# Splitting the second mixer's weights by two GpSimd transfers

## The chip, the cores and the metric

The kernel runs on one core of one Trainium2 chip. The metric is device time in microseconds (us) of one execution; lower is better. Engines are named as in the profile: PE is TensorE (matmul), PEld its weight loads, DVE is VectorE, ACT is ScalarE, POOL is GpSimd, SP is SyncE, which in the kernel before issues every transfer. Each engine executes its own instructions in the order in which the program wrote them, and waits on semaphores for what it needs.

## The reference

A two-layer backbone over 256 context and 512 latent tokens of width 1024, all in float32. Each layer scales and shifts its input, runs a mixer, adds the gated result to the residual, normalises, and then does the same with a gated feed-forward of 2816 hidden units. The first layer's mixer is linear attention beside differential attention; the second layer's is a bidirectional state-space mixer, and that is where the change lies:

```
z, xbc, dt = split(hh @ w_in, (2048, 2048 + 2 * 4 * 128, 2 * 32))
xbc = silu(conv5(xbc, conv_w) + conv_b);  xs, B, C = split(xbc)
y   = ssd(forward) + flip(ssd(backward)) + d_skip * xs
y   = group_rms_norm(y * silu(z)) ;  out = y @ w_out
```

Its input weights w_in have 5184 columns of 1024 rows; its output weights w_out have 2048 rows of 1024 columns.

## The kernel before, in words

**Three matmuls for one.** Activations and weights are float32, and a matmul runs on a rounded form of it (float32r). So each operand is held as two rounded halves: hi, the rounded value, and lo, the rest. `mm3` adds hi by hi, hi by lo and lo by hi. The activations stand in R0 in both halves; the weights are split block by block as they are needed.

**The weight stream.** Every weight block of the whole kernel stands in one list, `plan`, in the order in which it is used. A block is 128 partitions by up to 1024 columns, 512 KB: 128 columns of an input matrix (eight row groups), half of a 256-column piece (`plan_halves`, the "z" blocks), or 128 rows of an output matrix (`plan_rows`). `issue_loads` (line 373) moves the stream: up to three blocks ahead it issues a load by SP into one of the three RAW buffers; and when fewer than four blocks are issued and not freed, it writes the high half of the next one by a ScalarE copy and the low half by a subtraction on VectorE or GpSimd, into slot j % 4 of RW. `take` hands a block to the matmuls, and `free` says that its slot can be used again.

**The order of the work.** A planner, `Timing` (line 34), carries a cost for each operation on each engine. Each operation is given a planned start from its operands' planned times and the engine's free time; at the end of a stretch (`flush`) everything is emitted in the order of planned starts, and that order is each engine's program. `tm.either` puts an elementwise operation on VectorE or GpSimd, whichever ends sooner by plan. Matmuls are emitted in the order in which the Python code asks for them; between them `pump` and `settle` let *chains* go on, which are Python generators that yield what they wait for: tiles, a PSUM bank (`single_free`, `pair_free`) or a condition.

**The second mixer.** `layer1` follows a written order of projections:

```
ORDER1 = "b0 x0 z0 x1 z1 x2 b1 z2 x3 x4 o0 x5 z3 b2 z4 o1 z5 x6 b3 x7 z6 o2 p z7 o3"
```

Here b is B and C of a group (two blocks, "cv"), x is the input of four heads (two blocks, "cv"), z the gate of four heads (two half blocks, taken and freed as a pair), o the output product of a group of eight heads (four blocks "sw", all held through it and freed during its last half tile), p the preparation of the following norm. Before b0 stands one block "dt". In all 1 + 24 + 16 + 16 = 57 blocks. A projection is followed on VectorE by the five-tap convolution (`conv_out`); `states` makes the chunk states from weighted inputs (XW) and B; `y_tile` makes the output of one 128-token tile for four heads, multiplies by the gate and transposes into the output slots OT; `out_tile` multiplies those by the output weights. `LN.chain` normalises and writes the next layer's input. HX holds, at different times, CB, XW and a piece of the gate, and the first half of it is the norm's scratch.

**Names that the change touches:** `Timing.dma` (line 209), `RW` (line 237), `single` and `single_free` (lines 272 to 276), `issue_loads` (line 373), `LN.chain` (line 628), `gla_mix` (its two kv pairs), and in `layer1` `states`, `y_tile` and `free_of`.

Of the kernel before, what the change touches and what calls it, by code (L numbers as in the profile page):

```python
# [12 lines left out]
F32R = mybir.dt.float32r  # L13
U8 = mybir.dt.uint8
AF = mybir.ActivationFunctionType
ALU = mybir.AluOpType
# [17 lines left out]
class Timing:  # L34
# [174 lines left out]
    def dma(self, out, src):  # L209
# [4 lines left out]
        self.note([out], [src], end + 0.95)  # L214
        self.put(t, self.nc.sync.dma_start, (out, src), {})


@with_exitstack
def backbone(ctx: ExitStack, tc: tile.TileContext, ins: dict, out: bass.AP):
# [14 lines left out]
    LNS = pool.tile([P, 2, 16], F32, name="LNS")  # L234
    ea64 = pool.tile([P, 1], F32, name="ea64")
    R0 = pool.tile([P, 2, KD, NTOK], F32R, name="R0")
    RW = pool.tile([P, 8, 1024], F32R, name="RW")
    R0f, RWf = R0.bitcast(F32), RW.bitcast(F32)
    NU = 24
    HB = pool.tile([P, NU * U], F32, name="HB")  # L240
# [24 lines left out]
    def pair():  # L265

        return min((PS[:, i:i + 2, 0:384] for i in pair_banks[0] if i not in held), key=tm.free)

    def pair_free():
        return tm.free(pair())  # L270

    def single():
        return min((PS[:, 2 + i, :] for i in range(6) if 2 + i not in held), key=tm.free)

    def single_free():
        return tm.free(single())

# [43 lines left out]
    def need(*cs):  # L323
        while not all(c.done for c in cs):
            need_one()
# [43 lines left out]
    def plan_halves(key, n, w, c0):  # L369
        for i in range(2):  # L370
            plan.append(((key, n, i), [(None, w[i * 512:(i + 1) * 512, c0:c0 + 256].rearrange("(k p) c -> p k c", p=P))], (4, 256)))

    def issue_loads(limit=None):
        limit = limit or len(plan)
        while wq["loaded"] < min(limit, wq["issued"] + 3):
            j = wq["loaded"]
            _, pieces, (a, b) = plan[j]
            rv = RAW[:, j % 3, 0:a * b].rearrange("p (a b) -> p a b", b=b)
            for sl, ap in pieces:
                dma(rv[:, :, sl] if sl is not None else rv, ap)  # L380
            wq["loaded"] += 1
        if wq["issued"] < min(limit, wq["freed"] + 4):
            j = wq["issued"]
            _, _, (a, b) = plan[j]
            r = RAW[:, j % 3, 0:a * b]
            i = j % 4
            hi, lo, hf = RW[:, i, 0:a * b], RW[:, 4 + i, 0:a * b], RWf[:, i, 0:a * b]
            if plan[j][0] in wgate:
                tm.either(r, r, wgate[plan[j][0]], ALU.mult)
            S.activation(hi, r, AF.Copy)  # L390
            tm.either(lo, r, hf, ALU.subtract)
            wviews[j] = hi.rearrange("p (a b) -> p a b", b=b), lo.rearrange("p (a b) -> p a b", b=b)
            wq["issued"] += 1
            issue_loads(limit)
# [184 lines left out]
    class LN:  # L579


        def __init__(self, l, w, acc, src, dst, nxt, tiles, xr, tmp, gate, gb, nhx=2, banks=(6, 7)):
            self.t0, self.nhx, self.banks = tiles[0], nhx, banks
            self.l, self.w, self.acc, self.src, self.dst, self.nxt = l, w, acc, src, dst, nxt
            self.xr, self.tmp, self.gate, self.gb = xr, tmp, gate, gb

        def load_gates(self):
            for m, g in self.gate.items():
# [31 lines left out]
        def chain(self, t):  # L620
# [27 lines left out]
            gg, bb = GB[:, nl, nw, m, 0, :], GB[:, nl, nw, m, 1, :]  # L648
            hx = HX[:, t % self.nhx, :].rearrange("p (k c) -> p k c", c=P)
            quick = t >= self.t0 + self.acc.shape[1] - 2  # L650
            c = slice(t * P, (t + 1) * P)
            for hf in range(2):
                ks = slice(4 * hf, 4 * hf + 4)
# [173 lines left out]
    def layer0(mslots, RA, pre):  # L827
# [115 lines left out]
        def gla_mix(h):  # L943
# [19 lines left out]
            yield kdT, v, pair_free  # L963

            kv = []
            for half in range(2):
                q = pair()
                for c in range(6 * half, 6 * half + 6):
                    p = slice(64 * (c % 2), 64 * (c % 2) + 64)
                    o = q[:, c % 2, (c % 6) // 2 * P:((c % 6) // 2 + 1) * P]  # L970
                    mm(o, tiles(kdT)[p, c // 2, :], vt[p, c // 2, :], True, True)
                    kv.append(o)
# [386 lines left out]
    def layer1(lnin, lnc):  # L1359
# [211 lines left out]
        def states(hg):  # L1571
            xs = XS[hg % 2]
            cs = {}

            def weighted(n):
                xw = XW[ring("xw", 2)]
                ds = {2: slice(0, 1), 5: slice(1, 2)}.get(n, slice(0, 2))
                nd = ds.stop - ds.start
                V.tensor_tensor(xw[:, ds], heads(xs[:, n, :]).unsqueeze(1).to_broadcast([P, nd, 4, 64]),
                                tq(n, 2, hg)[:, ds].unsqueeze(3).to_broadcast([P, nd, 4, 64]), ALU.mult)  # L1580
                return xw, ds

            def product(n, xw, ds):
                o = single()
                mm(o[:, ds.start * 256:ds.stop * 256], Bt[:, n, :], xw[:, ds].rearrange("p d h c -> p (d h c)"), True, True)
                cs[n] = o.rearrange("p (d c) -> p d c", d=2)

            def recur(d, i):
                seq = ((0, 1, 2, 3, 4), (1, 0, 5, 4, 3))[d]
                order = ((2, 2, 3, 4, 5), (5, 5, 4, 3, 2))[d]  # L1590
                s2 = ST[:, order[i] - 2, d, :]
                if i == 0:
                    S.activation(s2, cs[seq[0]][:, d, :], AF.Copy)
                    return
                s, n = ST[:, order[i - 1] - 2, d, :], seq[i]
                f, j = head_rows(seq[i])
                dv = EAL[:, f, d * 32 + hg * 4:d * 32 + hg * 4 + 4, j].unsqueeze(2).to_broadcast([P, 4, 64])
                tm.either(heads(s2), heads(s), dv, ALU.mult)
                V.tensor_tensor(s2, cs[n][:, d, :], s2, ALU.add)

            for ns, rs in (((0, 1), ((0, 0), (1, 0), (0, 1), (1, 1))), ((5, 2), ((1, 2), (0, 2))), ((4, 3), ((1, 3), (0, 3), (1, 4), (0, 4)))):
                w = [weighted(n) for n in ns]
                yield w[0][0], w[1][0], single_free
                for n, x in zip(ns, w):
                    product(n, *x)
                for d, i in rs:
                    recur(d, i)

        def y_tile(hg, t):
# [24 lines left out]
            tm.either(A, R[:, 1], cb.unsqueeze(1).to_broadcast([P, 4, P]), ALU.mult)  # L1634
            co = DS[:, n % 3, :]
            V.scalar_tensor_tensor(co, tq(t, 1, hg)[:, 1, :], cbd, DB[:, hg * 4:hg * 4 + 4], ALU.mult, ALU.add)
            yield A, ST[:, t - 2], single_free
            yd = single()[:, 0:256]
            for h in range(4):
                mm(yd[:, h * 64:(h + 1) * 64], A[:, h, :], xs[:, t, h * 64:(h + 1) * 64], True, True)  # L1640
            of = single()
            for d in range(2):
                mm(of[:, d * 256:(d + 1) * 256], cs, ST[:, t - 2, d, :], True, True)
            yo = R[:, 1].rearrange("p h i -> p (h i)")
# [5 lines left out]
            tm.either(tt, tt, yo[:, 256:512], ALU.add)  # L1650
            V.tensor_tensor(tt, yd, tt, ALU.add)
            marks.add(("a", n))
            yield lambda: ("z", hg) in marks
            sz = SZ[hg % 2][(t - 2) // 2][:, (t % 2) * 256:(t % 2) * 256 + 256]
            V.scalar_tensor_tensor(sz, tt, 0.5, sz, ALU.mult, ALU.mult)
            S.activation(tt, sz, AF.Square, accum_out=SS[:, hg % 4, t - 2:t - 1])
# [14 lines left out]
        def free_of(hg, t):  # L1671

            if hg >= 6:
                return 7 in xsc
            if hg % 2 == 0:
                return hg == 0 or ("o", hg // 2 - 1, t) in marks
            return t < 4 or ("o", hg // 2, t - 2) in marks

        def ot(hg, t):

# [38 lines left out]
        ln = LN(1, 0, acc, x_res(1), x_res(2), (1, 1), range(2, NT), lnb1[0:1], [lnb1[2][:, 0:512], lnb1[2][:, 512:1024]], {0: lnb1[1]}, LNB[2:4], 1)  # L1719
        cvc = [None, None]  # L1720
        marks = set()
        need(*[lnc[t] for t in range(3)])
        dtc = dt_proj()
        low = pool.tile([P, P], F32, tag="mk1", name="low")
# [99 lines left out]
```

## Time and profile before

| | |
|---|---|
| median of three runs | 2057.66 us (2056.69 to 2058.1) |
| the profiled execution's own time | 2059.78 us |
| its span, first to last instruction | 2058.1 us |
| PE busy | 1925.8 us (94%) |
| DVE busy | 1380.8 us (67%) |
| ACT busy | 763.7 us (37%) |
| POOL busy | 230.6 us (11%) |
| bytes by SP's queue | 215.69 MB |

The stretches, in us from the span's start, are roughly: first mixer to 560, first feed-forward to 1040, the norm and then the second mixer to 1690, second feed-forward to 2058. In a row of the profile the tile names tell what is done: RAW is a loaded weight block, RW its two halves, R is R0, HB a large shared buffer, l a tile of the second mixer's ring slots (among them OT, XS and the gate), f one of a feed-forward's, PS is PSUM. Since a planner emits everything, all rows have one line number, 105; the tile names tell operations apart. `A<-B x24` is 24 instructions that write A from B; a number in brackets is the engine's idle time before, and what ended it.

### The profile page before, as it was taken

To read this page: it belongs to the slowest core of one execution; us is meant where nothing else is said; L and a number is where in the kernel's file an instruction comes from. 1 tells how busy PE (TensorE), PEld (TensorE's weight loads), DVE (VectorE), ACT (ScalarE), POOL (GpSimd) and SP (SyncE) were. 2 spreads that over 40 slices of the span, in tenths; PEclk is the share of its full clock that TensorE was granted. 3 is DMA by queue.
4 is the path that set the end of the run, shared out by engine and by line. 5 is a ranking of instruction groups with operands and counts; after the bars stand their busy time and mean duration, and the time that the engine had idled before them with its cause. 6 is when DMAs were issued, how large, how long until landed. Compare 5 with 4: busy or idle time off the path is not lost.

```text
span 2058.1 us, 27239 instructions
## 1 busy us (share of the span) xinstructions
PE 1925.8 (94%) x10660; PEld 1656.1 (80%) x10660; DVE 1380.8 (67%) x2096; ACT 763.7 (37%) x1470; POOL 230.6 (11%) x278
## 2 busy tenths in 40 slices
PE   7999999987999999999997998899998789999997
PEld 4877787966999989999986887787787678888886
DVE  3776656588725666566579998977978894443457
ACT  3523146445332221211243454545535443222232
POOL 0100000012200000000123321211202320000010
PEclk9999999999999999999998999999999899999999
DMA  8444311121524443443313332232233334333331
GB/s 280 121 131 134 113 51 31 44 80 61 174 65 131 133 142 122 127 153 117 118 49 126 98 88 88 62 88 88 85 100 98 101 97 152 102 107 102 94 115 60
DMA packets 233359, 217.42 MB, mean 106 GB/s; under 512 B 18901, under 2 KB 202839, under 8 KB 233231
## 3 DMA queue, kind: packets, MB, share of 16 engines
q1 hardware_dynamic: 233231, 215.69, 34.0%
q8 instruction: 83, 1.36, 0.3%
q14 instruction: 45, 0.37, 0.1%
HBM read 204.94 MB, written 10.72 MB: 105 GB/s over the span
## 4 chain that ended last, share of the span: by engine, by line
PE 71%; DVE 18%; ACT 3%; issue 3%; DMA 3%; POOL 1%; SPq 0%; POOLq 0%; DVEq 0%; ACTq 0%
PE PS L105 71%; DVE HB L105 12%; DVE RW L105 2%; ACT HB L105 2%; DVE l L105 1%; DMA HB<-acs_rows 1%; DMA HB<-in_x_dram 1%; DVE HX L105 1%; DVE LNS L105 1%; DVE sml L105 1%; ACT RW L105 1%; DMA HB<-in_mod_w_dram 0%; POOL LNS L105 0%; DVE R L105 0%; ACT R L105 0%
## 5 line engine op out<-in xcount | busy, mean ns | idle before, releaser
L105 PE MATMUL PS<-R,RW 128*128 128x384 f32 (+3 forms) x5184 | 987.1, 349 | 18.2 <-DVE l L105 5.9
L105 PEld LDWEIGHTS PS<-R,RW 128*128 128x128 f32 (+1 forms) x5184 | 888.1, 189 | 102.1 <-issue 22.7
L105 DVE TENSOR_TENSOR RW<-RAW,RW 128x1024 fp32r<-128x1024 f32 (+1 forms) x198 | 249.4, 1275 | 211.0 <-ACT RW L105 210.3
L105 ACT ACTIVATE RW<-RAW 128x1024 fp32r<-128x1024 f32 (+1 forms) x222 | 229.1, 1046 | 241.8 <-issue 181.1
L105 PE MATMUL PS<-RW,f 128*128 128x512 f32 x1320 | 304.6, 390 | 1.9 <-DVE RW L105 1.5
L105 PEld LDWEIGHTS PS<-RW,f 128*128 128x128 f32 x1320 | 247.0, 188 | 55.0 <-DVE RW L105 2.1
L105 ACT ACTIVATE HB<-PS 128x512 f32<-128x512 f32 (+4 forms) x247 | 129.6, 533 | 422.0 <-PE PS L105 414.5
L105 DVE TENSOR_TENSOR HB<-PS,HB 128x512 f32<-128x512 f32 (+2 forms) x276 | 160.6, 588 | 93.6 <-PE PS L105 89.6
L105 ACT ACTIVATE HB<-HB 128x128 f32<-128x128 f32 (+4 forms) x372 | 160.4, 490 | 127.9 <-DVE HB L105 85.4
L105 PE MATMUL PS<-RW,R 128*128 128x256 f32 (+1 forms) x1440 | 197.9, 296 | 6.3 <-DVE GB L105 4.5
L105 PEld LDWEIGHTS PS<-RW,R 128*128 128x128 f32 x1440 | 185.3, 194 | 14.2 <-issue 6.1
L105 PE MATMUL PS<-RW,l 128*128 128x512 f32 x576 | 159.0, 418 | 20.6 <-DVE RW L105 10.2
L105 DVE TENSOR_TENSOR HB<-HB 128x256 f32<-128x256 f32 (+4 forms) x196 | 162.2, 837 | 22.9 <-ACT HB L105 17.8
L105 PE MATMUL PS<-HB 128*128 128x128 f32 (+6 forms) x896 | 148.8, 352 | 10.9 <-DVE HB L105 7.6
L105 PEld LDWEIGHTS PS<-RW,l 128*128 128x128 f32 x576 | 106.4, 194 | 50.6 <-DVE RW L105 11.9
L105 PEld LDWEIGHTS PS<-HB 128*128 128x128 f32 (+3 forms) x896 | 102.9, 188 | 42.4 <-DVE HB L105 12.4
L105 POOL TENSOR_TENSOR HB<-HB 128x256 f32<-128x256 f32 (+1 forms) x54 | 73.0, 1364 | 510.6 <-DVE HB L105 362.5
L105 ACT ACTIVATE f<-HB 128x384 fp32r<-128x384 f32 (+2 forms) x68 | 37.4, 550 | 238.3 <-DVE HB L105 238.3
L105 DVE TENSOR_TENSOR HB<-HB,PS 128x384 f32<-128x384 f32 (+2 forms) x68 | 39.8, 585 | 104.9 <-PE PS L105 104.9
L105 DVE SCALAR_TENSOR_TENSOR HB<-HB,CW 128x770 f32<-128x770 f32 (+1 forms) x96 | 106.1, 1105 | 4.1
L105 PE MATMUL PS<-ident,HB 128*128 128x128 f32 x480 | 76.8, 287 | 30.7 <-DVE HX L105 14.0
L105 DVE SCALAR_TENSOR_TENSOR HB<-HB,CST 128x1024 f32<-128x1024 f32 x84 | 105.0, 1278 | 0.0
(145 smaller groups left out, 1306.8 us busy)
## 6 DMA issues: line engine op xcount, KB each, us to landing
RAW<-in_ffn_w_in_dram SPq DMA_DIRECT2D x88, 512.0 KB
HB<-in_mod_w_dram SPq DMA_DIRECT2D x48, 512.0 KB
RAW<-in_ffn_w_out_dram SPq DMA_DIRECT2D x44, 512.0 KB
RAW<-in_ssd_w_in_dram SPq DMA_DIRECT2D x40, 512.0 KB
mod<-in_mod_w_dram SPq DMA_DIRECT2D x72, 256.0 KB
HB<-acs_rows SPq DMA_DIRECT2D x64, 256.0 KB
RAW<-in_ev_w_in_dram SPq DMA_DIRECT2D x20, 512.0 KB
xres<-HB SPq DMA_DIRECT2D x16, 512.0 KB
```

The source lines that it names most:

```text
L105: f(*a, **k)
```

## The change

For the second mixer's blocks (keys "cv", "z", "sw" and "dt") nothing is loaded into RAW. GpSimd issues a transfer from DRAM straight into the high half, which rounds on the way; ScalarE writes the negated high half into the low half; GpSimd issues a second transfer of the same block from DRAM that adds onto the low half. All other blocks go as before. The ring has five slots in place of four, with two more buffers in RW. The area kept for the descriptors of GpSimd's transfers is set to 4096 bytes per partition.

Four waits are added: `states` and `y_tile` ask for two free PSUM banks ahead of their products, and take both at once; from the fifth head group on, `y_tile` waits for the output product that read the same sums of squares; `free_of` makes an odd head group's first two tiles wait for the last two of the output group before; and `LN.chain` of the mixer's norm waits until the last head group's products are laid out. In the first mixer the two kv pairs are chosen together.

```diff
+    def dma_cast(self, out, src, **add):
+        t = max(self.free(out, 1), self.ready(src, 1), self.floor.get("G", 0.0))
+        t = self.fit("G", t, 0.6)
+        cost = math.prod(out.shape) * 4 / 0.36e6
+        end = self.fit("D", t + 1.0, cost) + cost
+        self.note([out], [src], end + 0.95)
+        self.put(t, self.nc.gpsimd.dma_start, (out, src), add)
...
-    RW = pool.tile([P, 8, 1024], F32R, name="RW")
+    RW = pool.tile([P, 10, 1024], F32R, name="RW")
...
+    def singles(n):
+        return sorted((PS[:, 2 + i, :] for i in range(6) if 2 + i not in held), key=tm.free)[:n]
+
     def single():
-        return min((PS[:, 2 + i, :] for i in range(6) if 2 + i not in held), key=tm.free)
+        return singles(1)[0]
...
+    def second_free():
+        return tm.free(singles(2)[1])
...
+    def by_raw(j):
+        return plan[j][0][0] not in ("cv", "z", "sw", "d")
...
-        if wq["issued"] < min(limit, wq["freed"] + 4):
+        if wq["issued"] < min(limit, wq["freed"] + 5):
             j = wq["issued"]
...
+            i = j % 5
+            hi, lo, hf = RW[:, i, 0:a * b], RW[:, 5 + i, 0:a * b], RWf[:, i, 0:a * b]
+            if by_raw(j):
+                r = RAW[:, j % 3, 0:a * b]
+                if key in wgate:
+                    tm.either(r, r, wgate[key], ALU.mult)
+                S.activation(hi, r, AF.Copy)
+                tm.either(lo, r, hf, ALU.subtract)
+            else:
+                hv, lv = (x.rearrange("p (a b) -> p a b", b=b) for x in (hi, lo))
+                for sl, ap in pieces:
+                    tm.dma_cast(hv[:, :, sl] if sl is not None else hv, ap)
+                S.activation(lo, hf, AF.Copy, scale=-1.0)
+                for sl, ap in pieces:
+                    tm.dma_cast(lv[:, :, sl] if sl is not None else lv, ap, accum_op=ALU.add)
...
+            if self.ok is not None:
+                yield self.ok
...
-            for half in range(2):
-                q = pair()
+            for half, q in enumerate(sorted((PS[:, i:i + 2, 0:384] for i in pair_banks[0] if i not in held), key=tm.free)[:2]):
...
-                yield w[0][0], w[1][0], single_free
-                for n, x in zip(ns, w):
-                    product(n, *x)
+                yield w[0][0], w[1][0], second_free
+                for o, n, x in zip(singles(2), ns, w):
+                    product(o, n, *x)
...
-            yield A, ST[:, t - 2], single_free
-            yd = single()[:, 0:256]
+            yield A, ST[:, t - 2], second_free
+            yd, of = singles(2)
+            yd = yd[:, 0:256]
...
-            yield lambda: ("z", hg) in marks
+            yield lambda: ("z", hg) in marks and (hg < 4 or ("o", hg // 2 - 2, t) in marks)
...
-            return t < 4 or ("o", hg // 2, t - 2) in marks
+            g, u = (hg // 2 - 1, t + 2) if t < 4 else (hg // 2, t - 2)
+            return g < 0 or ("o", g, u) in marks
...
+        ln.ok = lambda: used(7)
...
-    nc = bacc.Bacc("TRN2", target_bir_lowering=False, num_devices=1)
+    nc = bacc.Bacc("TRN2", target_bir_lowering=False, num_devices=1, dynamic_dma_scratch_size=4096)
```

More of the change, by code (lines that the diff above doesn't have):

```diff
@@ L376, in issue_loads @@
             j = wq["loaded"]
[L377 to L380, printed above, removed]
+            key, pieces, (a, b) = plan[j]
+            if by_raw(j):
+                rv = RAW[:, j % 3, 0:a * b].rearrange("p (a b) -> p a b", b=b)
+                for sl, ap in pieces:
+                    dma(rv[:, :, sl] if sl is not None else rv, ap)
             wq["loaded"] += 1
-        if wq["issued"] < min(limit, wq["freed"] + 4):
+        if wq["issued"] < min(limit, wq["freed"] + 5):
             j = wq["issued"]
[L384 to L391, printed above, removed]
+            key, pieces, (a, b) = plan[j]
+            i = j % 5
+            hi, lo, hf = RW[:, i, 0:a * b], RW[:, 5 + i, 0:a * b], RWf[:, i, 0:a * b]
+            if by_raw(j):
+                r = RAW[:, j % 3, 0:a * b]
[8 more added lines that the diff above has]
+                S.activation(lo, hf, AF.Copy, scale=-1.0)
+                for sl, ap in pieces:
+                    tm.dma_cast(lv[:, :, sl] if sl is not None else lv, ap, accum_op=ALU.add)
             wviews[j] = hi.rearrange("p (a b) -> p a b", b=b), lo.rearrange("p (a b) -> p a b", b=b)
@@ L585, in __init__ @@
             self.xr, self.tmp, self.gate, self.gb = xr, tmp, gate, gb
+            self.ok = None
         def load_gates(self):
@@ L1581, in weighted, with product @@
                 return xw, ds
-            def product(n, xw, ds):
-                o = single()
+            def product(o, n, xw, ds):
                 mm(o[:, ds.start * 256:ds.stop * 256], Bt[:, n, :], xw[:, ds].rearrange("p d h c -> p (d h c)"), True, True)
@@ L1636, in y_tile @@
             V.scalar_tensor_tensor(co, tq(t, 1, hg)[:, 1, :], cbd, DB[:, hg * 4:hg * 4 + 4], ALU.mult, ALU.add)
-            yield A, ST[:, t - 2], single_free
-            yd = single()[:, 0:256]
+            yield A, ST[:, t - 2], second_free
+            yd, of = singles(2)
+            yd = yd[:, 0:256]
             for h in range(4):
                 mm(yd[:, h * 64:(h + 1) * 64], A[:, h, :], xs[:, t, h * 64:(h + 1) * 64], True, True)
-            of = single()
             for d in range(2):
```

## The prediction

> **What bounds the kernel now.** I read the page's totals first, then the busy time by stretch.
>
> ```profile
> span 2058.1 us, 27239 instructions
> ```
> ```profile
> core 0: us, PE busy (x) PEld busy (x) DVE busy (x) ACT busy (x) POOL busy (x), PEclk, DMA share, GB/s
> 0.00:560.00 560.00, 513.60 (x3214) 419.96 (x3215) 371.61 (x668) 226.13 (x452) 60.17 (x65) 0.97 0.35 111
> 560.00:1040.00 480.00, 480.00 (x2585) 449.04 (x2584) 268.97 (x302) 120.28 (x166) 10.75 (x6) 1.00 0.39 123
> 1100.00:1690.00 590.00, 528.37 (x3003) 451.33 (x3004) 512.47 (x842) 286.21 (x658) 125.64 (x179) 0.95 0.32 93
> ```
>
> From 560 to 1040 (the first feed-forward) TensorE never idles and has its full clock: nothing about weights can help there. The second mixer is 1100 to 1690. There TensorE idles 590 - 528.4 = 61.6 us and runs at clock 0.95, while VectorE is busy 87% of the time. All that the change touches lies in this stretch. The chain of waits and TensorE's own waits in it:
>
> ```profile
> by line: PE PS L105 37.8%; DVE HB L105 29.9%; issue 7.4%; ACT HB L105 5.0%; DVE l L105 4.9%; DVE RW L105 4.1%; DMA HB<-acs_rows 3.6%; DVE HX L105 2.0%; POOL HB L105 0.8%; DVE LNS L105 0.7%; DMA RAW<-in_ssd_w_in_dram 0.7%; ACT RW L105 0.5%;
> ```
> ```profile
> PE PS L105 <- DVE HB L105: 23.1, 18, 6.0
> PE PS L105 <- DVE l L105: 12.1, 8, 5.9
> PE PS L105 <- DVE HX L105: 9.2, 5, 4.0
> PE PS L105 <- DVE RW L105: 8.3, 3, 5.7
> PE PS L105 <- DVE GB L105: 4.5, 1, 4.5
> ```
>
> Every large wait names VectorE. Only 8.3 us name the split weights (RW); 23.1 + 12.1 + 9.2 = 44.4 us name VectorE's other results. So VectorE's lateness is the larger prize, and the weights' own path, which the change lengthens, is now nearly covered.
>
> **The change, part by part.** *Removed.* Before, a block of 512 KB comes by SP into RAW, ScalarE rounds it to the high half, and VectorE or GpSimd subtracts for the low half:
>
> ```profile
> L105 ACT ACTIVATE RW<-RAW 128x1024 fp32r<-128x1024 f32 x57 | 59.2, 1051 | 38.9 <-PE PS L105 20.3 <-issue 6.6 <-DMA RAW<-in_ffn_w_in_dram 6.1
> L105 DVE TENSOR_TENSOR RW<-RAW,RW 128x1024 fp32r<-128x1024 f32 x43 | 52.8, 1246 | 8.3 <-ACT RW L105 7.9
> L105 POOL TENSOR_TENSOR RW<-RAW,RW 128x1024 fp32r<-128x1024 f32 x14 | 35.3, 2526 | 81.3 <-ACT RW L105 81.3
> L105 POOL TENSOR_TENSOR RS<-RS,mhalf 128x1 f32<-128x1 f32 x16 | 9.3, 581 | 56.1 <-DVE RS L105 56.1
> L105 DVE TENSOR_SCALAR HB<-HB,CW,PRM 128x770 f32<-128x770 f32 x20 | 13.7, 684 | 3.0 <-ACT HB L105 3.0
> ```
>
> The selector takes the keys "d", "cv", "z" and "sw": 1 + 24 + 16 + 16 = 57 blocks, the mixer's output weights among them. A few of the 57 subtractions in this stretch belong to the next feed-forward; I take 40 of VectorE's 43 as removed: 40 x 1.246 = 50 us. GpSimd loses some 12 x 2.53 = 30 us. ScalarE is unchanged: the rounding copy becomes a negation of the same size, 1.05 us.
>
> VectorE's idle time goes from 590 - 512.5 = 77.5 to 127.5 us. If its lateness shrinks as its slack grows, the waits on it fall to 77.5/127.5 = 61%. Of the 44.4 us (with 1.4 us of two smaller groups, 45.8) that is **-17.9 us**; the bounds are 0 (the waits are lengths of dependent steps, not backlog) and -45.8.
>
> *Added: the path of a block.* Now a slot of the ring must first be free, then come a transfer by GpSimd that rounds, the negation, and a second transfer that adds. Before, the load sat in RAW ahead of time and only copy and subtraction followed. No transfer by GpSimd is in this trace; the nearest rows are SP's, from the chain in order of time:
>
> ```profile
> 1395.42 6.09 DMA HB<-acs_rows
> ...
> 1471.86 3.93 DMA RAW<-in_ssd_w_in_dram
> ```
>
> A 512 KB load took 3.93 us from issue to use. For each transfer I take that plus GpSimd's smallest arithmetic instruction, 0.58 us, as its issue: 2 x (3.93 + 0.58) + 1.05 = **10.1 us**. Lower end: issue hidden, 2 x 3.93 + 1.05 = 8.9. Upper end: the rounding one like the slow row, 6.09, the adding one twice a load since it reads two operands, 7.86, each issue as long as GpSimd's subtraction, 2.53, so 20.1 us. I take the low side, since the plain load is the same bytes and shape. The Trainium skill (DMA: Bandwidth & Descriptors, Anatomy of one DMA — SWDGE (gpsimd) path) gives 2.0 us plus bytes over 436 GB/s; my estimate from that page is 3.2 us each, a path of 7.5 us and a sum some 8 us lower. No run here shows it yet.
>
> *Where that path is exposed.* A slot freed one block at a time lies four blocks ahead, some 30 us, and covers 10 us. It is short where four output blocks (o0 to o3) are held together, or a pair (z). The matmul timeline at those places:
>
> ```profile
> 1296.99 1.05 ACT L105 ACTIVATE RW<-RAW 128x1024 fp32r<-128x1024 f32 x1
> ```
> ```profile
> 1306.84 2.43 PE L105 MATMUL PS<-RW,l 128*128 128x512 f32 x10
> 1314.99 1.22 PE L105 MATMUL PS<-RW,l 128*128 128x512 f32 x2 [5.72 <-DVE RW L105]
> ...
> 1418.73 5.64 PE L105 MATMUL PS<-RW,R 128*128 128x256 f32 x45
> ...
> 1425.52 2.19 PE L105 MATMUL PS<-RW,l 128*128 128x512 f32 x7
> 1429.70 1.04 PE L105 MATMUL PS<-RW,l 128*128 128x512 f32 x2 [1.99 <-DVE RW L105]
> ...
> 1471.43 6.36 PE L105 MATMUL PS<-RW,R 128*128 128x256 f32 x48
> ...
> 1566.85 1.31 PE L105 MATMUL PS<-RW,R 128*128 128x256 f32 x9
> ...
> 1575.21 2.33 PE L105 MATMUL PS<-RW,l 128*128 128x512 f32 x9 [1.37 <-DVE l L105]
> ...
> ```
> ```profile
> 1613.72 5.16 PE L105 MATMUL PS<-RW,l 128*128 128x512 f32 x21
> 1623.41 0.55 PE L105 MATMUL PS<-RW,R 128*128 128x256 f32 x1 [4.53 <-DVE GB L105]
> 1624.53 13.14 PE L105 MATMUL PS<-RW,R 128*128 128x256 f32 x95 [0.56 <-DVE RW L105]
> ...
> 1643.73 9.93 PE L105 MATMUL PS<-RW,R 128*128 128x512 f32 x33
> ```
> ```profile
> 1467.88 2.95 ACT L105 ACTIVATE RW<-RAW 128x1024 fp32r<-128x1024 f32 x3 [0.31 <-PE PS L105]
> ```
>
> With a ring of five, the fourth block of an output group needs the slot of the block before the last one ahead of it.
> - o0: that slot is free at 1296.99, so ready at 1307.1, before it is wanted (1309.3). The 5.72 us wait goes: **-5.7**.
> - o1: its slot is one of the z4 pair, freed at 1424.4: ready 1434.5 where matmuls now resume at 1429.70: **+4.8**.
> - z5: its second half uses the slot freed at 1467.88: ready 1478.0, wanted 12 matmuls after 1471.43, at 1473.0: **+5.0**.
> - o2: z6 ends at 1568.2, ready 1578.3, wanted at 1577.5: **+0.8**.
> - z7: first half waits in the fifth slot, second half's slot free three matmuls into the last twelve of the group begun at 1613.72, at 1616.7, ready 1626.8; 84 matmuls at 13.14/95 = 0.138 us then end at 1638.4, against 1637.7 now: **+0.7** (the 4.5 us put down to GB is in truth a wait for these weights too, since the subtraction stood right behind).
> - o3: z7 ends at 1637.7, ready 1647.8, wanted after six of the matmuls from 1643.73, at 1645.5: **+2.3**.
>
> Together **+7.9 us**. At 8.9 us the same list gives +2.3, at 20.1 us +65.7: each us on the path costs about 5.
>
> *GpSimd's queue.* Behind a transfer that waits for its slot or for the negation stand the padding clears that ScalarE's copies into the convolution wait for, the additions of the y tiles, and the reciprocal roots that VectorE waits for. GpSimd was busy 125.6 us of 590; minus 30, plus 114 issues of 0.58 = 66, it holds about 162. ScalarE, which almost never waited for a load, now has each negation behind one. I take **+3**, bounds 0 and 15 (a few late landings of some 4 us). SP sheds 57 loads; I count nothing, since its acs_rows loads are only 3.6% of the chain. Bytes: 28 MB read twice is +48 GB/s on 93, which by the same ratio takes the DMA share from 0.32 to about 0.49: not a bound.
>
> *Four buffer waits, banks.* Two wait for a second PSUM bank that the next product would have waited for anyway; the squares' wait and the output slot's lag work a group behind; the last holds the first norm until the last head's products are laid out. I take **+1**, bounds 0 and 6. The ordering of the two pair banks in the first mixer picks the same banks: 0, hidden by the work that already stands there. The ring of five outside the mixer: 0, TensorE is full there.
>
> *Sum.* -17.9 + 7.9 + 3 + 1 = -6.0 us of TensorE idle. The clock follows idling: 0.95 with 61.6 us idle, 1.00 with none, so 0.05 x 528 = 26 us lost, 0.43 us per idle us. -6.0 x 1.43 = **-8.6 us**. The profiled execution took 2059.8 us (span 2058.1 and 1.7 around it), 2.1 above the median of 2057.66. So 2051.2 in the profile's terms, **2049** against the median.
>
> **The rivals.** *Slow transfers (slower).* If a block's path exceeds 11.3 us, the new stalls outweigh the relief (-6.0 + 5 x 1.2 = 0), and o1, z5 and o3 show it. At 15 us: -6.0 + 24.5 = 18.5, x 1.43 = +26: 2084. For it: nothing here prices a transfer that rounds or adds, and one that adds reads twice. Against it: a plain one takes 3.93.
>
> *A draw.* VectorE's waits are lengths of dependent steps and shrink only by the 12 us that the additions eat: 2058. For it: VectorE idles 77.5 us even now.
>
> *A larger gain.* The subtractions are 4.1% of the chain, 24 us; if they leave it and the relief also comes, -42 + 12 = -30, x 1.43 = -43: 2015. Against it: the stretch's chain would turn to matmuls, 37.8% now, only if the rest shortened too.
>
> *VectorE holds up GpSimd's issues.* The convolution's first step takes 684 ns for 770 columns; if such an instruction keeps GpSimd from preparing a transfer, each of two waits up to 0.68 us, the path is 11.5 us, and -6.0 + 7 = +1: 2059. The Trainium skill has this as a rule (SBUF — State Buffer, SBUF: two separate sides): while VectorE runs in a mode that takes both shared ports, descriptors of GpSimd's transfers cannot be written. By it the gain is gone; no row here shows a transfer to test it on.
>
> **How the numbers follow.** Chances: the forecast (2040 to 2053) 0.38, slow transfers (2062 to 2100) 0.28, a draw 0.15, a larger gain 0.12, held-up issues 0.07. About 0.2%, 4 us, is what can be told from no change. Faster 0.38 + 0.12 = 0.50; same 0.15 and half of the last, 0.18; slower 0.28 and the other half, 0.32. The extreme ends, all relief or none with a path of 20.1 us, are some -60 and +124 us; I cut the range at 2020 and 2088, leaving about 0.13 out, and the likeliest case's own range is 2040 to 2053.
>
> **What would show it.** Right: VectorE near 460 us in the mixer, the waits on HB, l and HX nearer 28 us than 44, no 5.7 us wait in o0, and waits of some 5 us on RW at o1 and z5. Wrong: a path far from 10 us from slot to low half, RW waits above 20 us in all, GpSimd's arithmetic late behind its transfers, ScalarE waiting for landings, or VectorE's other waits unchanged.

## The result, and the profile after

The changed kernel takes **2144.45 us** (median; 2139.97 to 2147.93) against 2057.88 for the kernel before, beside it on the chip: ratio **1.0421** [1.0392, 1.0451], 4.2% slower. The forecast was 2049, the range 2020 to 2088.

The page of the changed kernel: its span, its totals, its two large DMA queues (packets, MB, share of 16 engines' span) and GpSimd's transfers (count, KB, median us from issue to landing).

```profile
span 2138.3 us, 27288 instructions
PE 1950.0 (91%) x10660; PEld 1675.0 (78%) x10660; DVE 1304.5 (61%) x2047; ACT 761.8 (36%) x1470; POOL 310.1 (15%) x384
q1 hardware_dynamic: 196479, 186.07, 27.9%
q0 software_dynamic: 73504, 59.25, 16.2%
RW<-in_ssd_w_in_dram POOLq DMA_DIRECT2D x80, 512.0 KB, 6.6
RW<-in_ssd_w_out_dram POOLq DMA_DIRECT2D x32, 512.0 KB, 5.6
```

VectorE has 76 us less to do (1380.8 to 1304.5; 50 were forecast), and the span is still 80.2 us longer. A block of 512 KB lands 5.6 to 6.6 us after its issue, and there are two such landings to a block. The queues also give the rates: q0 moved 59.25 MB in 16.2% of 2138.3 = 346 us of all engines, 171 GB/s; SP's q1 moved 186.07 MB in 597 us, 312 GB/s. By these shares a GpSimd transfer holds the DMA engines for 0.524 MB / 171 GB/s = 3.1 us, where one by SP holds them 1.7 us.

Busy time by stretch, changed kernel (the mixer now ends near 1770):

```profile
core 0: us, PE busy (x) PEld busy (x) DVE busy (x) ACT busy (x) POOL busy (x), PEclk, DMA share, GB/s
0.00:560.00 560.00, 512.43 (x3169) 416.64 (x3170) 367.03 (x665) 225.78 (x450) 62.94 (x67) 0.96 0.34 109
560.00:1040.00 480.00, 480.00 (x2586) 449.21 (x2585) 266.50 (x300) 119.47 (x165) 8.16 (x5) 1.00 0.39 124
1100.00:1770.00 670.00, 548.88 (x3006) 467.00 (x3005) 451.39 (x806) 288.40 (x670) 201.70 (x285) 0.91 0.63 124
```

The first two stretches are as before. All of the loss is in the mixer: 670 us where it was 590. TensorE's idle time there goes from 61.6 to 670 - 548.9 = 121.1 us (+59.5), and its busy time from 528.4 to 548.9, at a clock of 0.91 in place of 0.95.

What TensorE waited for in that stretch (us in total, times, longest), with the chain of waits by line under it:

```profile
PE PS L105 <- DVE HB L105: 29.5, 18, 5.6
PE PS L105 <- DMA RW<-in_ssd_w_in_dram: 21.2, 4, 9.5
PE PS L105 <- DVE HX L105: 20.9, 3, 16.0
PE PS L105 <- ACT HB L105: 13.0, 7, 2.9
PE PS L105 <- DMA RW<-in_ssd_w_out_dram: 11.8, 4, 6.7
PE PS L105 <- ACT R L105: 9.6, 2, 7.9
PE PS L105 <- DVE l L105: 7.1, 3, 4.5
```
```profile
by line: PE PS L105 25.8%; issue 25.5%; DMA RW<-in_ssd_w_in_dram 10.6%; DVE HB L105 7.9%; DMA RW<-in_ssd_w_out_dram 7.4%; POOL RW L105 4.3%; POOL HB L105 3.5%; ACT HB L105 3.2%; DVE l L105 2.6%; DMA HB<-acs_rows 2.0%; ACT RW L105 1.5%; ACT 
```

Two things are to be seen. TensorE now waits 21.2 + 11.8 = 33.0 us for weights themselves, eight times; before it was 12.8 (8.3 on RW and the 4.5 put down to GB), so weights are 20.2 of the 59.5 us of added idle time. And it still waits 57.5 us for VectorE (HB, HX, l), where it was to wait 28, although VectorE is busy only 451 of 670 us, and 13.0 + 9.6 = 22.6 us for ScalarE, where it waited 1.8 before: these two engines are held up in turn. The chain has turned from VectorE to transfers (18%) and to "issue" (25.5%), time in which an engine of the chain waited for nothing that the profile can name. Some of the waits of all engines around the mixer (1040 to 1760) say what holds them up:

```profile
POOL RW L105 <- ACT RW L105: 111.5, 27, 9.9
DVE HB L105 <- ACT HB L105: 102.6, 45, 9.5
ACT RW L105 <- DMA RW<-in_ssd_w_in_dram: 99.6, 33, 10.3
POOL RW L105 <- issue: 36.1, 10, 6.8
ACT RW L105 <- DMA RW<-in_ssd_w_out_dram: 33.8, 14, 7.2
DVE HB L105 <- POOL LNS L105: 22.5, 7, 17.9
```

ScalarE stands 99.6 + 33.8 = 133.4 us in front of negations whose rounding transfer has not landed; GpSimd stands 111.5 us in front of adding transfers whose negation isn't done, and 36.1 us, in ten pieces, at transfers with nothing to wait for. What was put behind them in those two queues comes late: VectorE waits 102.6 us for ScalarE's HB results, where it waited 29.6 before (1040 to 1690), and 22.5 us for GpSimd's roots. The mixer's first norm shows one such case whole: GpSimd, then VectorE, then TensorE in the changed kernel.

```profile
1091.14 1.62 POOL L105 DMA_DIRECT2D RW<-in_ssd_w_in_dram  x1 [3.27 <-ACT RW L105]
1098.04 1.57 POOL L105 DMA_DIRECT2D RW<-in_ssd_w_in_dram  x1 [5.28 <-issue]
1105.26 1.56 POOL L105 DMA_DIRECT2D RW<-in_ssd_w_in_dram  x1 [5.65 <-ACT HB L105]
1112.13 1.55 POOL L105 DMA_DIRECT2D RW<-in_ssd_w_in_dram  x1 [5.31 <-issue]
1113.04 1.24 POOL L105 TENSOR_TENSOR LNS<-LNS,mhalf 128x1 f32<-128x1 f32 x1
```
```profile
1114.31 5.30 DVE L105 TENSOR_SCALAR HB<-HB,LNS 128x1024 f32<-128x1024 f32 x1 [17.92 <-POOL LNS L105]
```
```profile
1119.99 1.97 PE L105 MATMUL PS<-ident,HB 128*128 128x128 f32 x8 [15.99 <-DVE HX L105]
```

A reciprocal root stands behind four transfers, three of which start 5.3 to 5.7 us after the one before has left GpSimd; VectorE waits 17.9 us for that root and TensorE 16.0 us for VectorE. The forecast named such roots, and priced all that stands behind transfers at 3 us together.

### The profile page after: what moved, and what is told of

Same layout as the page of the kernel before. It is cut to its first block, busy times and chain, and to the rows that moved or that the text cites. A ratio compares the mean times of both kernels' runs of the same rounds, so it can differ in the third digit from the quotient of the medians.

```text
span 2138.3 us, 27288 instructions
## 1 busy us (share of the span) xinstructions
PE 1950.0 (91%) x10660; PEld 1675.0 (78%) x10660; DVE 1304.5 (61%) x2047; ACT 761.8 (36%) x1470; POOL 310.1 (15%) x384
## 3 DMA queue, kind: packets, MB, share of 16 engines
q1 hardware_dynamic: 196479, 186.07, 27.9%
q0 software_dynamic: 73504, 59.25, 16.2%
## 4 chain that ended last, share of the span: by engine, by line
PE 67%; issue 9%; DVE 9%; DMA 8%; POOL 3%; ACT 3%; SPq 0%; POOLq 0%; ACTq 0%; DVEq 0%
PE PS L105 67%; DVE HB L105 5%; DMA RW<-in_ssd_w_in_dram 4%; DMA RW<-in_ssd_w_out_dram 2%; ACT HB L105 2%; POOL RW L105 1%; POOL HB L105 1%; DVE l L105 1%; ACT RW L105 1%; DVE LNS L105 1%; DVE RW L105 1%; DMA HB<-in_x_dram 1%; DMA HB<-acs_rows 1%; DVE sml L105 1%; DVE HX L105 0%
## 5 line engine op out<-in xcount | busy, mean ns | idle before, releaser
L105 PE MATMUL PS<-R,RW 128*128 128x384 f32 (+3 forms) x5184 | 1001.1, 352 | 40.7 <-DMA RW<-in_ssd_w_in_dram 11.1
L105 PEld LDWEIGHTS PS<-R,RW 128*128 128x128 f32 (+1 forms) x5184 | 899.0, 192 | 128.4 <-issue 22.3
L105 DVE TENSOR_TENSOR RW<-RAW,RW 128x1024 fp32r<-128x1024 f32 (+1 forms) x158 | 195.9, 1254 | 212.8 <-ACT RW L105 212.3
L105 ACT ACTIVATE RW<-RAW 128x1024 fp32r<-128x1024 f32 (+1 forms) x165 | 170.4, 1047 | 205.3 <-PE PS L105 128.8
L105 PE MATMUL PS<-RW,R 128*128 128x256 f32 (+1 forms) x1440 | 203.7, 301 | 25.1 <-DMA RW<-in_ssd_w_in_dram 16.6
L105 PEld LDWEIGHTS PS<-RW,R 128*128 128x128 f32 x1440 | 189.9, 198 | 33.4 <-issue 11.0
L105 ACT ACTIVATE HB<-HB 128x128 f32<-128x128 f32 (+4 forms) x372 | 160.0, 489 | 79.5 <-DVE HB L105 34.2
L105 PE MATMUL PS<-RW,l 128*128 128x512 f32 x576 | 160.3, 422 | 26.9 <-DMA RW<-in_ssd_w_out_dram 11.8
L105 DVE TENSOR_TENSOR HB<-HB 128x256 f32<-128x256 f32 (+4 forms) x192 | 154.5, 815 | 22.7 <-ACT HB L105 16.6
L105 POOL DMA_DIRECT2D RW<-in_ssd_w_in_dram x82 | 96.5, 1244 | 289.8 <-PE PS L105 114.6
L105 ACT ACTIVATE RW<-RW 128x1024 fp32r<-128x1024 f32 (+1 forms) x57 | 59.8, 1050 | 149.9 <-DMA RW<-in_ssd_w_in_dram 99.6
L105 PEld LDWEIGHTS PS<-ident,HB 128*128 128x128 f32 x480 | 59.2, 149 | 67.0 <-DVE HB L105 20.6
```

Source lines behind the costliest of these rows:

```text
L105: f(*a, **k)
```

## The experiments

All times are medians; the ratio is to the kernel before on the same chip, with its 95% interval. The runs come from several chips, beside which the kernel before took 2056.6 to 2058.9 us, and the intervals reach 2 to 7 us to either side; differences of a few us between two runs say little.

| run | us | ratio |
|---|---|---|
| the change | 2144.45 | 1.0421 [1.0392, 1.0451] |
| e1 no transfers by GpSimd | 2050.61 | 0.9969 [0.9958, 0.9980] |
| e11 e1 with the ring of four | 2058.41 | 0.9998 [0.9986, 1.0011] |
| e3 relief alone | 2027.95 | 0.9859 [0.9842, 0.9876] |
| e2 descriptor area 8192 | 2111.59 | 1.0266 [1.0249, 1.0284] |
| e8 small work off GpSimd | 2119.70 | 1.0305 [1.0285, 1.0325] |
| e4 plan by measured times | 2089.77 | 1.0162 [1.0145, 1.0179] |
| e12 landing alone | 2148.86 | 1.0446 [1.0411, 1.0481] |
| e13 issue alone | 2142.23 | 1.0410 [1.0381, 1.0438] |
| e17 issue and landing | 2113.23 | 1.0258 [1.0233, 1.0283] |
| e16 rate alone, half | 2091.33 | 1.0158 [1.0140, 1.0176] |
| e18 rate alone, two thirds | 2105.14 | 1.0233 [1.0204, 1.0263] |
| e5 e4 and area 8192 | 2078.82 | 1.0108 [1.0083, 1.0133] |
| e6 e5, single blocks only | 2035.21 | 0.9897 [0.9876, 0.9919] |
| e15 e5, single blocks and pairs | 2056.68 | 0.9992 [0.9977, 1.0008] |
| e9 e5, pairs and fours only | 2066.56 | 1.0045 [1.0027, 1.0062] |
| e10 the change, single blocks only | 2094.49 | 1.0192 [1.0172, 1.0213] |
| e14 e10 with area 8192 | 2074.98 | 1.0070 [1.0046, 1.0094] |
| e7 no adding transfer | 2045.64 | 0.9951 [0.9931, 0.9970] |

### The relief, the ring and the four waits: e1, e11, e3

e1 sends every block through RAW again; the ring of five, the four waits and the descriptor area stay. e11 is e1 with the ring of four.

```diff
-        return plan[j][0][0] not in ("cv", "z", "sw", "d")
+        return True
...
-        if wq["issued"] < min(limit, wq["freed"] + 5):
+        if wq["issued"] < min(limit, wq["freed"] + 4):
```

The first line is e1's and both together are e11's, whose slots are then j % 4 of RW's eight buffers.

> The changed kernel with every block by RAW again: ring of five, the four waits and the small descriptor area stay, no transfer by GpSimd. If the whole loss of 87 us is the transfers', this is 2050 to 2062 (ring of five takes away the waits on RW of 8 us before, the waits cost about 1). If the four buffer waits or the smaller area carry part of it, it is above 2070.

> No transfers by GpSimd, as in the run with all blocks by RAW, but with the ring of four; the four buffer waits stay. If the fifth slot is what gained 7 us there: 2055 to 2061. If the waits (or the bank choice that goes with them) gained it: 2048 to 2053.

e1: 2050.61. e11: 2058.41, no different from before. So the four waits (with the bank choice) cost nothing that can be measured, and the fifth slot alone is worth some 6 (by the ratios) to 8 us (by the medians). The whole loss belongs to the transfers and to the order that the planner writes with them.

e3 takes VectorE's subtraction away without a transfer: e1, with

```diff
-                tm.either(lo, r, hf, ALU.subtract)
+                if key[0] in ("cv", "z", "sw", "d"):
+                    S.activation(lo, hf, AF.Copy)
+                else:
+                    tm.either(lo, r, hf, ALU.subtract)
```

> Every block by RAW as in e1, but for the mixer's 57 blocks the low half is written by a ScalarE copy and the subtraction is left out (so the low half is not the rest of the weight): VectorE is relieved of the same work as in the changed kernel, with none of its path. If the waits on VectorE's other results shrink by 39%, as forecast, some 26 us below e1: 2025 to 2035. If they are lengths of dependent steps, within 8 us of e1.

2027.95, 22.7 us below e1. TensorE's waits on VectorE in e3, from 1040 to 1760:

```profile
PE PS L105 <- DVE HB L105: 19.7, 7, 8.1
PE PS L105 <- DVE l L105: 9.1, 6, 2.5
PE PS L105 <- DVE HX L105: 1.6, 2, 1.0
```

19.7 + 9.1 + 1.6 = 30.4 us. In e1 the same three make 53.2 in the same window, so they fell to 57%; the forecast said 61%. The relief is real, and of the size forecast, though e3 isn't a pure copy of it: its 57 copies keep ScalarE busy 55 us longer than in e1 (764.0 to 819.1). The transfers therefore cost 2144.45 - 2027.95 = **116.5 us** against a kernel that has the relief for nothing.

### The descriptor area: e2, e8

```diff
-dynamic_dma_scratch_size=4096)
+dynamic_dma_scratch_size=8192)
```

> The changed kernel with twice the descriptor area, 8192 bytes per partition, nothing else. Theory 'descriptor area': GpSimd sits some 5 us after a transfer with no releaser (36 us in the mixer) because the area is full, and all behind it is late: then those gaps vanish and the time falls by 25 to 60 us, to 2085 to 2120; the norm at the mixer's start no longer waits 16 us. Theory 'length of the path' (two landings of 6.6 us and a negation before a block can be used): within 10 us of 2144.

2111.59, 32.9 us less. In e2, from 1040 to 1760:

```profile
PE PS L105 <- DVE HX L105: 7.0, 4, 4.1
DVE HB L105 <- POOL LNS L105: 6.4, 8, 2.3
POOL RW L105 <- issue: 0.9, 3, 0.3
```

The stalls without a releaser fall from 36.1 to 0.9 us, VectorE's wait for the norm's root from 22.5 to 6.4, and TensorE's on HX from 21.8 to 7.0 in the same window. So the stalls are GpSimd waiting for room for descriptors, and the first norm's 16 us hang on them. They are only part of the chain's "issue" share, which is 25.8% in e2 too (1100 to 1770) and 7.5% in e5 below; what else stands in it is not shown.

e8 leaves the area small and takes the victims away: the padding clears go to VectorE, and so do the two reciprocal roots, as plain reciprocals with the root left out.

```diff
-            G.tensor_tensor(st[:, 15:16], st[:, 14:15], mhalf[:, 0:1], ALU.pow)
+            V.reciprocal(st[:, 15:16], st[:, 14:15])
...
-            G.memset(pre[:, z0:z0 + 2], 0.0)
+            V.memset(pre[:, z0:z0 + 2], 0.0)
...
-            G.tensor_tensor(r, r, mhalf[:, 0:1], ALU.pow)
+            V.reciprocal(r, r)
```

> The changed kernel with GpSimd's short instructions moved to VectorE: the padding clears, and in place of the two kinds of reciprocal root a reciprocal on VectorE (the root is left out). What remains on GpSimd are the transfers and the y tiles' additions. Theory 'short work late behind transfers in GpSimd's queue': 20 to 40 us less, 2105 to 2125, the 16 us wait at the mixer's first norm gone. Otherwise within 10 us of 2144.

2119.70, 24.8 us less, although GpSimd still stalls (43.4 us); TensorE's longest wait on HX falls from 16.0 to 4.0 us. Small work behind the transfers is a large part of how GpSimd's lateness reaches the end. Some of the gain may be the shorter step on VectorE itself.

### The planner's numbers: e4, e12, e13, e17, e16, e18, e5

The changed kernel's planner believes in 0.6 us to issue, 0.36 MB per us (1.46 us for 512 KB) and a landing some 3.4 us after the issue. e4 tells it what the profile measured:

```diff
+        issue, land = (0.8, 5.6) if len(out.shape) < 3 or out.shape[1] == 1 else (1.3, 6.6)
-        t = self.fit("G", t, 0.6)
+        t = self.fit("G", t, issue)
-        cost = math.prod(out.shape) * 4 / 0.36e6
-        end = self.fit("D", t + 1.0, cost) + cost
+        cost = math.prod(out.shape) * 4 / 0.18e6
+        end = max(self.fit("D", t + 1.0, cost) + cost, t + land - 0.95)
```

> The changed kernel with the planner told what the trace shows of a transfer: GpSimd held 1.3 us (0.8 for output weights), landing 6.6 us (5.6) after issue, half the rate on the wires; it had 0.6 and 3.4 us. The work is the same, only the orders on the engines change. Theory 'wrong plan' (transfers stand too early in GpSimd's and ScalarE's queues, and what stands behind waits): at least 25 us less, 2090 to 2120. Theory 'length of the path' or 'descriptor area': within 12 us of 2144.

2089.77, 54.7 us less from another order of the same work (7 of some 2430 elementwise instructions also move from GpSimd to VectorE). Which of the three numbers does it? Each was told alone, and issue and landing together. The one that matters most, e16's, is a single line (e18 has 0.24e6); e12 has the landing's line of e4 without the others, e13 the issue's.

```diff
-        cost = math.prod(out.shape) * 4 / 0.36e6
+        cost = math.prod(out.shape) * 4 / 0.18e6
```

> The planner is told the measured landings (6.6 and 5.6 us) but keeps the change's issue time of 0.6 us and its transfer rate. If late landings at the in-order queues are what the wrong plan costs: 2085 to 2105, about as with all measured times (2089.8). If the issue time is: 2125 to 2148, as the change.

> The planner is told the measured issue times (1.3 and 0.8 us) but keeps the change's landing and rate. The mirror of the run before: 2125 to 2148 if late landings are the cost, 2085 to 2105 if GpSimd's issue time is.

> The planner is told measured issue and landing times together, and keeps the change's rate. If the rate decides: 2130 to 2150. If issue and landing only help together: 2085 to 2105.

> The planner is told half the transfer rate (0.18 in place of 0.36 MB per us, so that transfers that follow one another are planned 2.9 us apart and not 1.5), and keeps the change's issue and landing numbers. If the rate is what the wrong plan costs, since neither issue nor landing alone changed anything: 2085 to 2105. If only all three together help: 2125 to 2150.

> As the run with the rate alone, but two thirds of it (0.24 MB per us, 2.2 us apart). If the spacing works by degree: half way between the change's 2144 and the run with half the rate, some 2105 to 2130. If it has a point from which it works: near one of the two.

Landing alone 2148.86 and issue alone 2142.23: my two theories of this point both fell. The rate alone does all of it, 2091.33, and two thirds of the rate gives 2105.14: 1.46, 2.18 and 2.91 us per transfer give 2144, 2105 and 2091. Three orders that get better with the spacing make an accident of one order unlikely, though the middle one lies at the fast end of what was expected. Issue and landing together give 2113.23, which I had expected of neither theory; that they space the transfers in another way, and so get part of it, is my reading and not shown. In e16, from 1040 to 1760:

```profile
ACT RW L105 <- DMA RW<-in_ssd_w_in_dram: 46.4, 19, 7.5
PE PS L105 <- DMA RW<-in_ssd_w_in_dram: 22.8, 6, 9.6
PE PS L105 <- DMA RW<-in_ssd_w_out_dram: 22.4, 7, 6.6
ACT RW L105 <- DMA RW<-in_ssd_w_out_dram: 11.8, 7, 3.1
```

ScalarE's standing time falls from 133.4 to 58.2 us, while TensorE's own waits for weights do not fall (45.2 us, where they were 39.5 in the change in this window). What falls is its waiting for other engines' results: on VectorE (HB, HX, l) from 53.7 to 31.6 us, on ScalarE (HB, R) from 22.6 to 10.4. GpSimd's stalls without a releaser stay (36.3 to 34.1 us), but VectorE's wait for the norms' roots halves (22.5 to 11.2) and its wait for ScalarE's HB falls from 102.6 to 64.7. So the gain is in what is queued behind the transfers and the negations; that the planner, with nearly the true spacing, puts each negation where its transfer has landed is my reading of it.

e5 joins e4 and e2:

> The changed kernel with both mends: the planner's measured times of e4 (-55 us) and the area of 8192 bytes of e2 (-33 us). If the two losses are separate: about 2057. If they are the same loss seen twice (the wrong plan was what stood behind the full area): 2080 to 2090. What then remains above e3's 2028 is the path itself, two landings just before use.

2078.82: of the 54.7 and 32.9 us, 65.6 together. So 22.0 us, two thirds of what the area is worth, are the same loss, late work in the queues of GpSimd and ScalarE, reached from two sides; with the better order the area is worth 11 us more. In e5, from 1040 to 1760, TensorE waits for VectorE's results 34.2 us in all, as in e3 (34.0), and for weights 34.8 us, where e3 has none. The relief is there in full, and by this count the path of the blocks is nearly all that sets e5 50.9 us above e3: 34.8 times the forecast's 1.43 is 49.8.

### Which blocks: e6, e15, e9, e10, e14

With measured times and the larger area (e5), the transfers are kept for some kinds of block only, by `by_raw`: "cv" and "d" are the 25 blocks freed one at a time, "z" the 16 in pairs, "sw" the 16 held in fours.

```diff
-        return plan[j][0][0] not in ("cv", "z", "sw", "d")
+        return plan[j][0][0] not in ("cv", "d")
```

This is e6; e15 names "cv", "d" and "z", e9 "z" and "sw".

> e5 with transfers for the 25 blocks that are used and freed one at a time (dt and cv); the 32 blocks of the gate and of the output weights, which are held in pairs and fours, go by RAW again. Theory 'path exposed where blocks are held together': those 25 cost nothing and relieve VectorE by some 22 us of work, so 2035 to 2047, below e1 (2050.6). Theory 'any transfer in GpSimd's queue costs': above 2060.

> Measured times, area 8192; transfers for single blocks and for the gate's pairs, output weights by RAW. If pairs and fours cost alike (TensorE's waits on them are 21.0 and 20.5 us in the run with held blocks alone): half way between 2035.2 and 2078.8, 2050 to 2064. If the fours alone cost: 2035 to 2045. If the mixing with single blocks costs: 2068 to 2080.

> Transfers only for the 32 blocks that are held in pairs or fours (z and output weights), with measured planner times and the 8192-byte area; the 25 single blocks go by RAW. Held-blocks theory (a block whose slot comes free together with others has too little lead for a path of two landings): the loss stays, 2080 to 2098. Rival, the loss goes with the number of transfers whatever the block: 2040 to 2060.

e6 is **2035.21**, 1.0% faster than the kernel before and 15.4 us below e1, where 25/57 of the relief would be 10: no cost of the path can be seen for single blocks. Pairs add 21.5 us (e15, 2056.68, the half way expected), fours another 22.1. But held blocks alone (e9, 2066.56) lose only 16.0 us against e1, not the 29 or more that I expected: the loss isn't the sum of its kinds, and some 28 us of it (2078.82 - 2066.56 + 15.4) come only when single and held blocks go by the same queue. TensorE's waits for weights, e6 first and then e9, 1040 to 1760:

```profile
PE PS L105 <- DMA RW<-in_ssd_w_in_dram: 6.6, 1, 6.6
```
```profile
PE PS L105 <- DMA RW<-in_ssd_w_in_dram: 21.0, 5, 8.1
PE PS L105 <- DMA RW<-in_ssd_w_out_dram: 20.5, 3, 7.4
```

The direct stalls on weights sit at the held blocks. Does that mean that the plan and the area matter only there? e10 is the change with e6's line alone, e14 has the larger area besides.

> Transfers only for the 25 single blocks, but with the planner's numbers and the 4096-byte area of the change. If a wrong plan and a full area cost in proportion to the transfers: 2035 + 66 x 25/57 = about 2064 (2055 to 2072). Rival, they cost only where blocks are held together: within 2033 to 2045.

> Transfers only for the 25 single blocks, planner's numbers as in the change, area 8192 bytes. Between 2035.2 (measured times and 8192) and 2094.5 (neither) it says which of the two costs that 59 us. If the full area (28 us of GpSimd's stalls there) strikes the first norm and its followers: 2055 to 2072. If the plan: 2080 to 2095. If the area is all: 2035 to 2045.

No. Single blocks alone, with the change's numbers and area, take 2094.49, 59 us above e6 and beyond both theories: almost the whole 65.6 us of plan and area, with 25 blocks of 57. Of the 59, taken in this order, the area accounts for some 20 (e14) and the plan for some 40. TensorE hardly waits for weights in e10 (5.5 us); GpSimd's stalls (28.1 us) and the first norm's 16 us on HX are there again. TensorE waits 81.1 us for VectorE (HB, HX, l) where it is 30.8 in e6, and VectorE, from 1040 to 1760, waits for GpSimd's HB results besides its roots:

```profile
DVE HB L105 <- POOL HB L105: 20.0, 4, 15.7
```

In e6 that is 0.2 us. So that loss does not go with the number of transfers, nor with held blocks: 25 blocks are enough to hold up what stands behind them.

### The adding transfer: e7

```diff
-                for sl, ap in pieces:
-                    tm.dma_cast(lv[:, :, sl] if sl is not None else lv, ap, accum_op=ALU.add)
```

> The changed kernel with the adding transfer left out (so the low half holds the negated high half): half of the transfers, half of the path (one landing and the negation, some 8 us), nothing else changed. Theory 'length of the path' at 5 us for each us: from 15 us to 8, some 35 us x 1.4 less, 2090 to 2100; with the area no longer full another 20, down to 2070. Theory 'ScalarE's queue waits for the rounding transfer': little gain, above 2115.

2045.64, 98.8 us less, more than I expected of half the transfers: a second landing on every path, the second wait in GpSimd's queue and half the descriptors all go (its stalls without a releaser fall from 36.1 to 0.8 us, with the small area). The run doesn't tell these apart. Its page:

```profile
q0 software_dynamic: 36752, 29.63, 6.6%
RW<-in_ssd_w_in_dram POOLq DMA_DIRECT2D x40, 512.0 KB, 5.1
```

The rounding transfers alone hold the engines for 6.6% of this run's span of 2043.7 = 135 us, 220 GB/s. Taken from the change's 346 us, the adding ones hold them for 211 us, 140 GB/s; this is a difference of two kernels, not a reading.

## Why the prediction was wrong, point by point

**Relief, -17.9 us of idle: right.** Times its factor it is -26; e3 against e1 shows -22.7 us of time and, over the whole span, -17.7 us of idle (125.0 to 107.3). So close a match is partly luck, since e3 also loads ScalarE. The draw and the larger gain (2015) are both out: the waits were no mere dependent steps, and the relief is no more than forecast.

**Path of a block, 10.1 us: mis-sized.** The term took a plain load's 3.93 us for both transfers. Landings are 6.6 and 5.6 us. For z7's second half GpSimd's queue reads

```profile
1688.75 0.84 POOL L105 DMA_DIRECT2D RW<-in_ssd_w_in_dram  x1 [2.24 <-PE PS L105]
...
1694.81 1.33 POOL L105 DMA_DIRECT2D RW<-in_ssd_w_in_dram  x1 [3.36 <-ACT RW L105]
```

and TensorE goes on at 1703.21: 14.5 us from the free slot, above the 11.3 from which the slow-transfers rival decides. The list of places was good, with one place missing:

```profile
1360.67 2.80 PE L105 MATMUL PS<-RW,l 128*128 128x512 f32 x11 [0.26 <-DMA RW<-in_ssd_w_out_dram]
...
1409.33 9.85 PE L105 MATMUL PS<-R,RW 128*128 128x256 f32 x46 [4.66 <-DMA RW<-in_ssd_w_in_dram]
...
1482.49 5.03 PE L105 MATMUL PS<-RW,l 128*128 128x512 f32 x11 [4.57 <-DMA RW<-in_ssd_w_out_dram]
...
1530.64 5.65 PE L105 MATMUL PS<-RW,R 128*128 128x256 f32 x26 [6.06 <-DMA RW<-in_ssd_w_in_dram]
...
1654.48 5.89 PE L105 MATMUL PS<-RW,l 128*128 128x512 f32 x16 [6.68 <-DMA RW<-in_ssd_w_out_dram]
...
1703.21 11.64 PE L105 MATMUL PS<-RW,R 128*128 128x256 f32 x83 [9.54 <-DMA RW<-in_ssd_w_in_dram]
```

o0's 5.7 us went (0.26 is left), 4.7 us at 1409, between o0 and o1, were not on the list, o1 waits 4.6 (+4.8 forecast), z5 6.1 (+5.0), o2 6.7 (+0.8), z7 9.5 (+0.7), o3 none on weights (+2.3). All waits on weights make 33.0 us; before, with the one put down to GB, they were 8.3 + 4.5 = 12.8. So the term is +20.2, not +7.9. That is within what I had allowed between its ends.

**GpSimd's queue, +3 us, bounds 0 and 15: this is the step that failed.** I priced the late followers in GpSimd's and ScalarE's queues as a few late landings. I took the issue as 0.58 us; the groups of the changed kernel have

```profile
L105 POOL DMA_DIRECT2D RW<-in_ssd_w_in_dram x82 | 96.5, 1244 | 289.8 <-PE PS L105 114.6 <-ACT RW L105 74.8 <-ACT HB L105 51.4
L105 POOL DMA_DIRECT2D RW<-in_ssd_w_out_dram x32 | 24.0, 760 | 81.4 <-ACT RW L105 36.7 <-PE PS L105 28.9 <-ACT HB L105 14.5
```

But the issue time isn't what cost: telling the planner of it gained nothing (e13). By the trace TensorE waits 87.1 us in the mixer for results of VectorE (60.7, with 3.2 of two smaller groups), ScalarE (22.6) and GpSimd (3.8); the forecast's terms leave some 34 for these, 28 of them VectorE's and 4 for this term and the four waits. So the term of 3 came out near 56. What cost is the order written by a planner that believed in twice the true rate (53.1 us, e16), and an area for descriptors too small for the transfers (32.9 us, e2), 65.6 us together (e5), some 46 us of idle by the forecast's factor. The rate stood in the diff, as 0.36 MB per us, and I never set it against a price of my own; the 4096 bytes stood there too and had no term at all. I had seen the ingredient ("ScalarE now has each negation behind one") and put no number on it.

**Four waits +1, other stretches 0: right**, by e11 and by the windows. **The clock's factor** was 1.43; 59.5 us more idle made 80.2 us more span, 1.35.

**The rivals.** Slow transfers was the right side, and its price stands close to e5, where the relief is whole and little but the path is left: 2084 at 15 us against 2078.82 measured. The closeness is partly luck: e5 runs in another order, and TensorE waits 34.8 us for weights there, 22 more than before, where the rival's price makes it 32 more. The change itself is 60 us worse than that rival's price; no rival had the plan. VectorE's holding up of GpSimd's issues, at 0.07, is not what stalls GpSimd here: in e2 VectorE does the same work and the stalls are gone. The rule of the Trainium skill for it (SBUF — State Buffer, SBUF: two separate sides) is neither borne out nor refuted by any run here beyond that. The formula of the Trainium skill (DMA: Bandwidth & Descriptors, Anatomy of one DMA — SWDGE (gpsimd) path) gives 3.2 us for 512 KB, and by my estimate from it the change would have been faster (the prediction's list comes out 11 us lower at a path of 7.5 us, not 8); the traces have 5.1 us for rounding alone (e7) and 5.6 to 6.6 where half of the transfers add, and the measurement decides.

**The chances.** 0.32 lay on slower, but the range's upper end was cut at 2088 although the extreme end, +124 us, had been worked out. The bound of 15 on the queue was the unfounded one: no row supported it.

**What stays open.** Why single and held blocks together cost some 28 us more than each by itself: in the profiled executions (e5 and e1 against e6 and e9) it is 24.6 us, of which 15.2 are longer matmuls and only 9.4 idle time, so it isn't mainly waiting. Why issue and landing told together gain 31 us when each alone gains nothing. And what the chain's "issue" share is beside GpSimd's stalls.

## What to carry to other kernels

When work moves to an engine that executes in program order, price what stands behind each of its waits, not the waits alone: here TensorE's own waits for the new transfers were the smaller part. Where a planner writes the order, its cost numbers are part of the change; set each of them against a measured row before you trust the order; here the rate was the one that counted. A longer path from a free slot showed no cost for buffers that come free one at a time (6.6 us of waits on weights in e6), once plan and area were right, and a plain one where several are held and freed together (41.5 us in e9). Here the split is worth keeping for the first kind only, at 2035.21 us.

## What the runs showed of the hardware

- **Rate.** Transfers that GpSimd issues moved 171 GB/s where SP's moved 312 in the same kernel; 220 for those that round (e7), and, by subtraction, 140 for those that add.
- **Issue time goes with the pieces.** GpSimd's queue on the pages of e6 (50 transfers) and of e15 (82) reads

```profile
q0 software_dynamic: 52000, 25.69, 8.8%
```
```profile
q0 software_dynamic: 68896, 42.47, 13.2%
```

  With the change's 73504 packets for 114 transfers, a single block's transfer has 1040 packets, a pair's (68896 - 52000)/32 = 528 and an output block's 144. All three move 512 KB. In e6, which has only the first kind, one takes GpSimd 1.31 us on the mean and lands in 6.8 us; in e9 a pair's takes 1.07 and 6.2 us, an output block's 0.79 and 5.6. Whether it rounds or adds counts as well: in e7, with rounding transfers alone, the means are 0.86 for the first two kinds together and 0.57 for the last, against 1.24 and 0.76 in the change.
- **A descriptor area too small for the transfers stalls GpSimd for several us at a transfer** (36.1 us in ten stalls, the longest 6.8). The profile names no releaser for it ("issue"); with 8192 bytes in place of 4096 it is gone (36.1 to 0.9 us), and with half the transfers too (0.8, e7). The Trainium skill (Perfetto Trace Analysis, DMA Instruction — SWDGE (GPSIMD)) says that a DMA engine may begin on descriptors before GpSimd has written the last of them, above all when there are more than the buffer holds. No run here shows when the engines begin; the page gives no price for a buffer that is too small, and the price here is in e2.
